# First norm of a two-layer decoder step: all squares on ScalarE behind the token splits, and half of the first key products in other PSUM banks

## The chip, the core and the metric

The kernel runs on one core of a Trainium2 chip. The metric is the device time of one execution in microseconds. Three runs of the kernel before gave 1672.52 us at the median (1671.01 to 1674.88). The engines are TensorE (PE, with its weight loads PEld), VectorE (DVE), ScalarE (ACT), GpSimd (POOL) and SyncE (SP), which here issues nearly all DMAs. Each works through its own instructions strictly in order.

## The reference

One inference step of a trunk of two layers for 512 prompt tokens and 32 sample tokens that share the weights. Only the start matters here:

```python
def rms_norm(x, g):
    y = xf * lax.rsqrt(jnp.mean(xf * xf, axis=-1, keepdims=True) + RMS_EPS)
    return (y * g).astype(x.dtype)

for l in range(DEPTH):
    hp = rms_norm(xp, norm_mix[l]); hs = rms_norm(xs, norm_mix[l])
    if l % 2 == 0:
        z, xbc, dt, q, k, v = even_split(hp @ w_in_even[li])
        ...   # state space branch, sliding-window attention, output projection
    else:
        ...   # forgetting attention
    ...       # cross-attention, SwiGLU
```

Layer 0 is the even one: its norm is the first norm, and the keys `k`, the values `v` (computed together with `dt`) and the queries `q` are its first projections.

## The kernel before

Tokens lie along the free axis: 544 of them (512 and 32), in two chunks of 256 and 288 columns (`CH`), called c0 and c1. The 1024 model features are eight tiles k0 to k7 of 128 partitions; k0 to k3 and k4 to k7 sit in two buffers each ("halves"). All products are done in 32-bit: each operand is split into a high part (a cast to `fp32r`, ACT) and a low part (the rest, DVE), and `acc3` (L187, its matmuls recorded at L138) issues three matmuls for each k: high by high, high by low, low by high. For activations `split` (L248) makes `xh` at L258 and `xl` at L259; for weights `wpiece` (L161) loads a piece of 512 KB into one of two raw buffers, L169 makes the high and L170 the low part. `vpieces` (L174) does the same for the value weights (L182, L183).

The norm's gain is put into the split; the factor 1/rms comes later, at the eviction from PSUM. For it the squares of all eight k are added into `acc`, TensorE sums each over the partitions by matmuls with one column (`rstd`, L290), DVE scales the sum (L302), POOL raises it to the power -0.5 (L303, called the power below), TensorE spreads it over the partitions (the matmuls on `room,col`), and DVE copies that to SBUF (L310). Only then can the key products be evicted (L462).

`first` (L392) is the opening. Its DMAs are tied into one order: x of c0, k0 to k3; key weights 0; x of c0, k4 to k7; key weights 1; x of c1 in two halves; the table of constants `cst`. Each x load is followed by four splits. Then `setup_copies` makes 16-bit copies of the identity and of the mask on DVE (L371, L372), and a loop over c0 and c1 makes the squares: those of c0 by POOL (L429), those of c1 by ACT (L431) through two buffers `sq`, all additions by POOL (L433). `norm_end` stands in `with self.ahead(m0)`, which gives it the priority of the kernel's start.

`even` (L644) goes on: `linear` makes the keys (two weight pieces by two chunks, 24 matmuls each), the value products follow (five blocks of tokens, 24 matmuls with 272 columns each), then the queries. A product takes one PSUM bank; the pool gives four banks to the tag `tr`, three to `sc` (the attention's scores), two to `tp`, one to `pv`. Keys and values all use `tr`.

The program text sets priorities only: `build` opens the context with `schedule_with_timeline_sim=True`, and the scheduler orders each engine's instructions by a timeline of its own. `after` (L451) adds a dependence that holds for this order alone, without a semaphore. So an edit at the start can also reorder instructions far behind it. The stretch concerned here is the end of the state space branch at 330 to 420 us: the prompt's scan (L870 to L903), the sample's state update (L991 loads the state into `hb`, POOL scales it at L1002, DVE adds at L1003, L1004 stores it), and beside it the split of the memory tokens (`mem`, `memh`, `meml`) and their keys.

Of the kernel before, what the change touches and what calls it, by code (L numbers as in the profile page):

```python
# [9 lines left out]
F32 = mybir.dt.float32  # L10
# [4 lines left out]
AF = mybir.ActivationFunctionType  # L15
ALU = mybir.AluOpType
# [3 lines left out]
P = 128  # L20
D = 1024
KD = 8
# [24 lines left out]
C_ID, C_U, C_L, C_ONE, C_SWA, C_MS, C_MN = 0, 128, 256, 384, 512, 768, 896  # L47
C_UB, C_LB, C_S4, C_BLK, C_OH, C_PW, C_END = 1024, 1056, 1088, 1120, 1128, 1144, 1145
# [58 lines left out]
class Net:  # L107
# [79 lines left out]
    def acc3(self, ps, whi, wlo, xhi, xlo, first, last):  # L187
        self.mm(ps, whi, xhi, first, False)
        self.mm(ps, whi, xlo, False, False)
        self.mm(ps, wlo, xhi, False, last)  # L190

    def linear(self, get, ns, KT, xh, xl, evac, tail=0, lead=0, order=(0, 1)):

        for _ in self.linear_steps(get, ns, KT, xh, xl, evac, tail, lead, order):
            pass

    def linear_steps(self, get, ns, KT, xh, xl, evac, tail=0, lead=0, order=(0, 1), tag="tr"):
        def run(n, c, w):
            o, N = CH[c]
            ps = self.psum(tag, [P, 288])  # L200
            for k in range(KT):
                self.acc3(ps[:, 0:N], w[0][:, k], w[1][:, k], xh[k][:, o:o + N], xl[k][:, o:o + N],
                          k == 0, k == KT - 1)
            evac(n, c, ps[:, 0:N])
        ns = list(ns)
        groups = [ns[:lead]] if lead else []
        groups += [[n] for n in ns[lead:len(ns) - tail]]
        groups += [ns[len(ns) - tail:]] if tail else []
        for g in groups:
            ws = [get(n) for n in g]  # L210
            for c in order:
                for n, w in zip(g, ws):
                    run(n, c, w)
                    yield
# [152 lines left out]
    def setup_copies(self):  # L367
        nc, c = self.nc, self.cst
        self.identb = self.keep(64).bitcast(BF16)
        self.maskb = self.keep(128).bitcast(BF16)  # L370
        nc.vector.tensor_copy(self.identb, self.ident)  # L371
        nc.vector.tensor_copy(self.maskb, c[:, C_SWA:C_SWA + 256])  # L372
        self.half = self.keep(60)
        nc.vector.tensor_scalar(self.half, self.par[:, V_CW:V_CW + 60], 0.5, None, ALU.mult)
        self.nsink = self.keep(17)
        nc.vector.tensor_scalar(self.nsink, self.par[:, V_SK:V_SK + 17], -1.0, None, ALU.mult)
# [15 lines left out]
    def first(self):  # L392

        nc, I = self.nc, self.I
        self.x = Big(self, "x")
        st = self.norm_begin(G_MIX)
        m0 = self.mark()
        d = None

        def load(*a):  # L400
            nonlocal d
            e = nc.sync.dma_start(*a)
            d = self.after(e, d) if d is not None else e

        def x_in(c, m):
            o, N = CH[c]
            load(self.x.half(m)[:, :, o:o + N], I["x"][:, 4 * m:4 * m + 4, o:o + N])
            for k in range(4 * m, 4 * m + 4):
                self.last = self.split(st["h"], st["l"], self.x[k][:, o:o + N], k, o, N, self.par[:, G_MIX + k:G_MIX + k + 1])
        x_in(0, 0)  # L410
        self.whold = d
        self.early = self.wpiece(I["we_k"][0], KD, 128)
        d = self.wlast
        x_in(0, 1)
        self.whold = d
        self.early1 = self.wpiece(I["we_k"][1], KD, 128)
        d = self.wlast
        x_in(1, 0)
        x_in(1, 1)
        load(self.cst, I["cst"])  # L420
        self.whold = None
        self.setup_copies()
        for c, (o, N) in enumerate(CH):
            acc = st["acc"][:, o:o + N]
            for k in range(KD):
                x = self.x[k][:, o:o + N]
                sq = acc if k == 0 else self.pers.tile([P, 288], F32, tag="sq", bufs=2, name=self.nm("sq"))[:, 0:N]
                if c == 0:
                    nc.gpsimd.tensor_tensor(sq, x, x, ALU.mult)  # L429
                else:  # L430
                    nc.scalar.activation(sq, x, AF.Square)  # L431
                if k:
                    nc.gpsimd.tensor_tensor(acc, acc, sq, ALU.add)  # L433
            with self.ahead(m0):
                self.norm_end(st, c)
        return st

    def mark(self):
# [205 lines left out]
    def even(self, st, nxt, fill):  # L644
        nc, tc, I, O = self.nc, self.tc, self.I, self.O
        with ExitStack() as es:
            ev = es.enter_context(tc.tile_pool(name="even", bufs=1))
            kT = ev.tile([P, 2, NT], F32, name="kT")
# [3 lines left out]
            dtA = ev.tile([P, 5, 16], F32, name="dtA")  # L652
            craw = ev.tile([P, 12, 27], F32, name="craw")
            xh, xl = st["h"], st["l"]
            self.linear(lambda n: self.early1 if n else self.early, range(2), KD, xh, xl, self.scale_evac(lambda n: kT[:, n], st["b"]))

            wv = self.vpieces(I["we_v"])
            nc.gpsimd.memset(dt, 0.0)
            for i, (o, w) in enumerate(TB):
                ps = self.psum("tr", [P, 288])  # L660
                for k in range(KD):
                    whi, wlo = wv[k // 4][0][:, k % 4], wv[k // 4][1][:, k % 4]
                    a, b = xh[k][:, o:o + w], xl[k][:, o:o + w]
# [19 lines left out]
            with tc.tile_pool(name="swa", bufs=1) as self.sw, tc.tile_pool(name="conv", bufs=1) as cv:  # L683
# [11 lines left out]
                m0 = self.mark()  # L695
# [11 lines left out]
            with tc.tile_pool(name="ssm", bufs=1) as sm:  # L707

                oh, ol = Big(self, "oh", F32R), Big(self, "ol", F32R)
                for c in range(2):  # L710
                    o, N = CH[c]
# [79 lines left out]
    def ssm(self, xs, BC, dt, dtA, sm):  # L791
        nc, I, O = self.nc, self.I, self.O
# [11 lines left out]
        oh = sm.tile([P, 16], F32R, name="ohs")  # L804
        self.zero(cs2.bitcast(F32))
        self.zero(ecs2.bitcast(F32))
        nc.vector.tensor_copy(oh, self.cst[:, C_OH:C_OH + 16])
        self.after(nc.vector.tensor_copy(sel, self.cst[:, C_OH:C_OH + 16].rearrange("p (j r) -> p j r", r=2).unsqueeze(3).to_broadcast([P, 8, 2, 64])), self.last)
        hs_ = sm.tile([P, 2048], F32, name="hst")
        h, csT, ecsT = hs_[:, 0:1024], hs_[0:16, 1024:1536], hs_[0:16, 1536:2048]  # L810
        ps = self.psum("tp", [P, 512])
# [8 lines left out]
        ps = self.psum("tp", [P, 4, 64])  # L820
# [9 lines left out]
        for c in range(4):  # L830
            o = 128 * c
            tok = slice(o, o + 128)
            xx = self.H("xdt")[:, 0:2048].rearrange("p (s h x) -> p s h x", s=2, h=16)
# [3 lines left out]
            ps = self.psum("tp", [P, 4, 128])  # L837
# [6 lines left out]
            for g in range(2):  # L844
                ps = self.psum("tp", [P, 8, 64])
# [6 lines left out]
            for g in range(2):  # L852

                sct = []
                for f in range(2):
# [6 lines left out]
                    for e in range(4):  # L862
                        x = slice(128 * e, 128 * e + 128)
# [13 lines left out]
                for j in range(4):  # L877
                    x = xs[4 * g + j][:, tok]
# [1005 lines left out]
```

## Time and profile before

| | |
|---|---|
| median of three runs | 1672.52 us |
| the profiled execution | 1674.47 us, its span 1672.7 us |
| PE, PEld busy | 1630.3 us (97%), 1522.7 us (91%) |
| DVE, ACT, POOL busy | 1195.0, 795.4, 339.7 us |
| the key products | first matmul at 7.68 us, last begins at 29.02 us |
| the value products and the two sums beside them | 31.02 to 49.34 us |
| first query product | at 49.34 us |

The profile page gives totals by engine, and one digit (tenths of busy time) for each fortieth of the span, here 41.8 us long. The trace answers narrower questions: who waited for whom, the timeline of one engine with the idle time before an instruction in brackets, the chain of waits, and the busy time, granted clock and DMA share of chosen stretches. A PE row's length is modelled and overlaps the next row, so a matmul's cost is read from the distance of the starts.

### The profile page before, as it was taken

How to read it: one execution, taken by the hardware profiler on the slowest of the kernel's cores; microseconds unless marked ns; L12 is line 12 of the kernel's file. 1: busy time of each engine (PE TensorE's matmuls, PEld its weight loads, DVE VectorE, ACT ScalarE, POOL GpSimd, SP SyncE). 2: the span in 40 equal slices, each digit the busy share in tenths (PEclk: the TensorE clock that was granted, in tenths of full speed). 3: DMA queues.
4: the chain of work that ended last, by engine and by line, in shares of the span. 5: the costliest groups of instructions: out<-in, count | busy, mean ns of one | idle time of the engine just before them, and what ended most of it. 6: DMA issues, size and time to landing. Idle time of an engine off the chain costs nothing.

```text
span 1672.7 us, 32467 instructions
## 1 busy us (share of the span) xinstructions
PE 1630.3 (97%) x12720; PEld 1522.7 (91%) x12720; DVE 1195.0 (71%) x2322; ACT 795.4 (48%) x1637; POOL 339.7 (20%) x511
## 2 busy tenths in 40 slices
PE   7999999999999999999999998998999999999998
PEld 6999999877998999999999995655989999999997
DVE  6678889777776876767666577655667886767654
ACT  4367645344545444444445265544545444444434
POOL 6022323675422300000002203111313200000002
PEclk9999999998999999999999999999999999999999
DMA  5121243156433242323224434555451232323222
GB/s 188 56 64 52 83 153 130 39 183 223 160 115 115 64 131 91 101 89 110 80 77 136 133 108 122 161 165 190 139 190 51 94 112 92 104 87 108 76 71 85
DMA packets 71221, 189.27 MB, mean 113 GB/s; under 512 B 7612, under 2 KB 34012, under 8 KB 63452
## 3 DMA queue, kind: packets, MB, share of 16 engines
q1 hardware_dynamic: 69932, 185.43, 33.7%
q8 instruction: 100, 1.64, 0.4%
q10 hardware_dynamic: 1056, 1.24, 0.3%
q0 software_dynamic: 80, 0.52, 0.1%
q14 instruction: 53, 0.43, 0.1%
HBM read 172.22 MB, written 14.95 MB: 112 GB/s over the span
## 4 chain that ended last, share of the span: by engine, by line
PE 90%; DVE 3%; POOL 2%; issue 2%; DMA 1%; ACT 1%; SPq 0%; POOLq 0%; DVEq 0%; ACTq 0%
PE ps L138 65%; PE ps L1594 22%; PE ps L141 3%; POOL room L433 1%; DMA o_s_ssm<-hb 0%; DVE meml L259 0%; DVE xs L910 0%; POOL sq L429 0%; ACT prt L1192 0%; DVE prt L1191 0%; SPq L1268 0%; POOL E L870 0%; DMA room<-wo_d 0%; DMA x<-x 0%; DVE ol L256 0%
## 5 line engine op out<-in xcount | busy, mean ns | idle before, releaser
L138 PE MATMUL ps<-xh,split_t 128*128 128x288 f32 (+1 forms) x2304 | 464.5, 294 | 9.6 <-ACT split_t L169 7.7
L138 PEld LDWEIGHTS ps<-xh,split_t 128*128 128x128 f32 x2304 | 372.4, 191 | 11.9 <-ACT split_t L169 7.7
L1594 PE MATMUL ps<-xf,split_t 128*128 128x272 f32 x2592 | 350.4, 289 | 0.1
L138 PE MATMUL ps<-xl,split_t 128*128 128x256 f32 (+1 forms) x1152 | 339.4, 295 | 1.1 <-DVE xl L259 1.0
L1594 PEld LDWEIGHTS ps<-xf,split_t 128*128 128x128 f32 x2592 | 335.9, 188 | 0.5 <-DVE split_t L1575 0.5
L268 POOL TENSOR_TENSOR room<-room,sq 128x256 f32<-128x256 f32 (+1 forms) x96 | 87.2, 912 | 771.4 <-ACT sq L267 769.8
L138 PEld LDWEIGHTS ps<-xl,split_t 128*128 128x128 f32 x1152 | 219.6, 191 | 3.5 <-DVE xl L259 1.9
L138 PE MATMUL ps<-hh,fs 128*128 128x256 f32 (+1 forms) x1024 | 209.4, 290 | 3.6 <-DVE fs L1640 3.6
L169 ACT CAST split_t<-room 128x1024 fp32r<-128x1024 f32 (+1 forms) x128 | 130.3, 1019 | 154.2 <-PE ps L138 116.9
L170 DVE TENSOR_TENSOR split_t<-room,split_t 128x1024 fp32r<-128x1024 f32 (+1 forms) x128 | 159.1, 1245 | 33.5 <-ACT split_t L169 32.8
L138 PEld LDWEIGHTS ps<-hh,fs 128*128 128x128 f32 x1024 | 166.5, 190 | 4.3 <-DVE fs L1640 4.0
L1574 ACT CAST split_t<-fr 128x1024 fp32r<-128x1024 f32 x108 | 113.5, 1052 | 111.8 <-PE ps L1594 52.6
L1575 DVE TENSOR_TENSOR split_t<-fr,split_t 128x1024 fp32r<-128x1024 f32 x108 | 131.8, 1220 | 37.2 <-ACT split_t L1574 36.9
L138 PE MATMUL ps<-hl,fs 128*128 128x256 f32 (+1 forms) x512 | 147.9, 290 | 0.0
L138 PE MATMUL ps<-oh,split_t 128*128 128x288 f32 (+1 forms) x512 | 105.5, 295 | 1.3 <-ACT oh L253 1.2
L138 PEld LDWEIGHTS ps<-hl,fs 128*128 128x128 f32 x512 | 97.0, 190 | 0.0
L138 PEld LDWEIGHTS ps<-oh,split_t 128*128 128x128 f32 x512 | 82.1, 188 | 6.2 <-ACT oh L253 3.0
L138 PE MATMUL ps<-ol,split_t 128*128 128x288 f32 (+1 forms) x256 | 75.4, 294 | 0.3 <-DVE ol L256 0.2
L259 DVE SCALAR_TENSOR_TENSOR xl<-x,room,xh 128x256 fp32r<-128x256 f32 (+1 forms) x96 | 69.7, 755 | 5.4 <-ACT xh L258 5.4
L138 PE MATMUL ps<-hh,split_t 128*128 128x256 f32 (+1 forms) x384 | 73.5, 289 | 0.0
L1639 ACT CAST fs<-room 128x512 fp32r<-128x512 f32 x64 | 39.6, 619 | 67.1 <-PE ps L138 58.9
L1575 DVE TENSOR_TENSOR fs<-fr,fs 128x512 fp32r<-128x512 f32 x36 | 24.9, 691 | 64.9 <-ACT fs L1574 64.9
(427 smaller groups left out, 3158.2 us busy)
## 6 DMA issues: line engine op xcount, KB each, us to landing
fr<-wfi SPq DMA_DIRECT2D x36, 1024.0 KB
room<-wfo SPq DMA_DIRECT2D x64, 256.0 KB
room<-wo_e SPq DMA_DIRECT2D x16, 512.0 KB
xk<-mem_k SPq DMA_DIRECT2D x8, 1024.0 KB
xv<-mem_v SPq DMA_DIRECT2D x8, 1024.0 KB
room<-wfi SPq DMA_DIRECT2D x16, 512.0 KB
fox_k<-fox_k SPq DMA_DIRECT2D x64, 128.0 KB
fox_v<-fox_v SPq DMA_DIRECT2D x64, 128.0 KB
```

Of the source, the lines that this page charges most:

```text
L138: return self.placed(self.nc.tensor.matmul(out, lhsT, rhs, start=start, stop=stop))
L141: return self.placed(self.nc.tensor.transpose(out, in_, self.ident[0:k, 0:k]))
L169: nc.scalar.copy(hi[:, 0:n], raw[:, 0:n])
L170: nc.vector.tensor_tensor(lo[:, 0:n], raw[:, 0:n], hi[:, 0:n].bitcast(F32), ALU.subtract)
L259: return nc.vector.scalar_tensor_tensor(ll, src, g, hh.bitcast(F32), ALU.mult, ALU.subtract)
L268: nc.gpsimd.tensor_tensor(acc, acc, sq[:, 0:N], ALU.add)
L433: nc.gpsimd.tensor_tensor(acc, acc, sq, ALU.add)
L1574: nc.scalar.copy(hi, t)
L1575: nc.vector.tensor_tensor(lo, t, hi.bitcast(F32), ALU.subtract)
L1594: self.nc.tensor.matmul(ps, w[a][:, k], x[:, b, k], start=start and k == 0 and i == 0, stop=k == 3 and i == 2, skip_group_check=True)
L1639: nc.scalar.copy(hi, raw)
```

## The change

Squares: POOL's multiplications go. All sixteen squares are made by ACT, into `xx`, which has a place for each k, and they are tied behind the last split of the tokens (`self.last` is the last `xl`); the order of the additions on POOL is tied from c0 to c1, and `norm_end` loses its raised priority. The two 16-bit copies and the small copy `ohs`, which belongs to a later stage, are tied behind `self.last` too. Keys: `lead=2` makes `linear` take both weight pieces together, so that the order is c0 of both, then c1 of both, and the first two products take banks with the tag `sc`, the other two `tr`.

```diff
-    def linear(self, get, ns, KT, xh, xl, evac, tail=0, lead=0, order=(0, 1)):
+    def linear(self, *a, **k):
...
-            ps = self.psum(tag, [P, 288])
+            ps = self.psum(tag() if callable(tag) else tag, [P, 288])
...
-        nc.vector.tensor_copy(self.identb, self.ident)
-        nc.vector.tensor_copy(self.maskb, c[:, C_SWA:C_SWA + 256])
+        self.after(nc.vector.tensor_copy(self.identb, self.ident), self.last)
+        self.after(nc.vector.tensor_copy(self.maskb, c[:, C_SWA:C_SWA + 256]), self.last)
...
+        xx = Big(self, "xx")
         for c, (o, N) in enumerate(CH):
             acc = st["acc"][:, o:o + N]
             for k in range(KD):
-                x = self.x[k][:, o:o + N]
-                sq = acc if k == 0 else self.pers.tile([P, 288], F32, tag="sq", bufs=2, name=self.nm("sq"))[:, 0:N]
-                if c == 0:
-                    nc.gpsimd.tensor_tensor(sq, x, x, ALU.mult)
-                else:
-                    nc.scalar.activation(sq, x, AF.Square)
+                sq = xx[k][:, o:o + N] if k else acc
+                self.after(nc.scalar.activation(sq, self.x[k][:, o:o + N], AF.Square), self.last)
                 if k:
-                    nc.gpsimd.tensor_tensor(acc, acc, sq, ALU.add)
-            with self.ahead(m0):
-                self.norm_end(st, c)
+                    i = nc.gpsimd.tensor_tensor(acc, acc, sq, ALU.add)
+                    if c and k == 1:
+                        self.after(i, summed)
+                    summed = i
+            self.norm_end(st, c)
...
-            self.linear(lambda n: self.early1 if n else self.early, range(2), KD, xh, xl, self.scale_evac(lambda n: kT[:, n], st["b"]))
+
+            turn = iter(("sc", "sc", "tr", "tr"))
+            self.linear(lambda n: self.early1 if n else self.early, range(2), KD, xh, xl, self.scale_evac(lambda n: kT[:, n], st["b"]), lead=2,
+                        tag=lambda: next(turn))
...
-        nc.vector.tensor_copy(oh, self.cst[:, C_OH:C_OH + 16])
+        self.after(nc.vector.tensor_copy(oh, self.cst[:, C_OH:C_OH + 16]), self.last)
```

ScalarE in the opening, before. `xh` of 288 columns are the splits of c1, L431 the squares, `vh` the value weights, `split_t` the pieces of key and query weights.

```order
L258 ACTIVATE xh_81<-x_79,room 128x288 x4
L431 ACTIVATE room<-x_79 128x288
L258 ACTIVATE xh_96<-x_94,room 128x288 x4
L431 ACTIVATE sq_164<-x_79 128x288
L431 ACTIVATE sq_167<-x_79 128x288
L182 CAST vh_310<-vr_309 128x1088
L431 ACTIVATE sq_170<-x_79 128x288
```

The same place after the change (lines have moved by a few; L428 are the squares).

```order
L258 ACTIVATE xh_81<-x_79,room 128x288 x4
L258 ACTIVATE xh_96<-x_94,room 128x288 x4
L428 ACTIVATE room<-x_79 128x256
L428 ACTIVATE xx_133<-x_79 128x256 x3
L428 ACTIVATE xx_140<-x_94 128x256 x4
L428 ACTIVATE room<-x_79 128x288
L428 ACTIVATE xx_133<-x_79 128x288 x3
L428 ACTIVATE xx_140<-x_94 128x288 x4
L169 CAST split_t<-room 128x1024
L182 CAST vh_298<-vr_297 128x1088
L169 CAST split_t<-room 128x1024
L182 CAST vh_298<-vr_297 128x1088
```

The sixteen squares stand in one run behind the splits, and the first value weights behind them and behind the first query piece.

TensorE between the last key product and the first value products, before. `ps_283` is the last key product, `room,col_78` spreads the factor of c0, `128x2x128` adds the attention's mask into a bank of scores, `128x1` are the sums of the squares of c1, `ps_319` is the first value block.

```order
L138 MATMUL ps_159<-room,col_78 128x128 x2
L138 MATMUL ps_283<-xh_96,split_t 128x288
L138 LDWEIGHTS room
L138 MATMUL ps_1441<-room 128x2x128
L138 LDWEIGHTS room
L138 MATMUL ps_1468<-room 128x2x128
L138 LDWEIGHTS room
L138 MATMUL ps_1501<-room 128x2x128
L138 MATMUL ps_185<-room 128x1 x3
L138 MATMUL ps_319<-vh_310,xh_81 128x272
L138 MATMUL ps_319<-vh_310,xl_82 128x272
L138 MATMUL ps_319<-vl_311,xh_81 128x272
```

After the change, the same place. `ps_271` is the last key product, `ps_149` the sums of c0, `ps_307` and `ps_334` the first two value blocks.

```order
L138 MATMUL ps_271<-xh_96,split_t 128x288
L138 LDWEIGHTS room
L138 MATMUL ps_1429<-room 128x2x128
L138 MATMUL ps_149<-room 128x1 x2
L138 MATMUL ps_307<-vh_298,xh_81 128x272
L138 MATMUL ps_307<-vh_298,xl_82 128x272
L138 MATMUL ps_334<-vh_298,xh_81 128x272
L138 MATMUL ps_334<-vh_298,xl_82 128x272
L138 MATMUL ps_307<-vl_299,xh_81 128x272
```

The sums of c1 have left this place: they and two of the three masks stand behind the first two value blocks now, and the spread of c0's factor stands inside these, after 28 value matmuls. The first value block has changed places with them and waits for the value weights alone.

SyncE in the state space branch, before. `wxk` are weight pieces for the memory keys, `hb` the sample's state, `o_p_ssm` the store of the prompt's final state, `mem` the memory tokens.

```order
L165 DMA room<-wxk 128x1024 x3
L991 DMA hb_4377<-state 128x1024 x2
L991 DMA hb_4487<-state 128x1024 x2
L903 DMA o_p_ssm<-hst 128x1024
L165 DMA room<-wxk 128x1024
L991 DMA hb_4626<-state 128x1024 x2
L1338 DMA mem_4643<-mem 128x512 x4
```

And after.

```order
L165 DMA room<-wxk 128x1024 x2
L905 DMA o_p_ssm<-hst 128x1024
L165 DMA room<-wxk 128x1024
L993 DMA hb_4365<-state 128x1024 x2
L993 DMA hb_4475<-state 128x1024 x2
L165 DMA room<-wxk 128x1024
L993 DMA hb_4614<-state 128x1024 x2
```

The store and one weight piece have moved ahead of the first four loads of the state; on DVE the addition on which the store waits has moved ahead of the products `sxdt` (L949) too.

## Rows read from the trace of the kernel before

**Rows 1.** The page: busy time by engine, and TensorE's granted clock in forty slices (9 is 0.9 or more).

```profile
PE 1630.3 (97%) x12720; PEld 1522.7 (91%) x12720; DVE 1195.0 (71%) x2322; ACT 795.4 (48%) x1637; POOL 339.7 (20%) x511
PEclk9999999998999999999999999999999999999999
```

**Rows 2.** The chain of waits, cut off at 60 us: start, length, what.

```profile
28.43 0.79 POOL room L433
...
31.02 29.09 PE ps L138 x217
```

**Rows 3.** Stretches of the opening: length, then busy time (and instructions) of PE, PEld, DVE, ACT and POOL, granted clock, DMA share, GB/s.

```profile
10.40:15.85 5.45, 5.42 (x25) 5.43 (x26) 5.45 (x6) 3.85 (x9) 5.29 (x7) 1.00 1.04 420
15.85:22.70 6.85, 5.77 (x41) 5.04 (x40) 6.85 (x11) 4.55 (x8) 6.09 (x7) 1.00 0.34 115
22.70:26.10 3.40, 3.34 (x14) 3.34 (x15) 3.40 (x6) 2.12 (x4) 1.61 (x1) 0.50 0.02 5
29.50:32.90 3.40, 2.11 (x18) 1.88 (x16) 1.99 (x5) 1.04 (x1) 2.16 (x3) 1.00 0.43 154
32.90:36.30 3.40, 3.40 (x18) 3.40 (x17) 0.29 (x1) 0.00 (x0) 1.01 (x1) 0.51 0.50 154
```

**Rows 4.** TensorE's timeline: start, length, instruction, in brackets the idle time before it and what ended it.

```profile
7.68 0.58 PE L138 MATMUL ps<-xh,split_t 128*128 128x256 f32 x1 [7.68 <-ACT split_t L169]
10.43 0.80 PE L138 MATMUL ps<-xh,split_t 128*128 128x256 f32 x2 [1.95 <-DVE split_t L170]
12.94 0.41 PE L138 MATMUL ps<-xl,split_t 128*128 128x256 f32 x1
13.58 0.41 PE L138 MATMUL ps<-xl,split_t 128*128 128x256 f32 x1
16.29 0.28 PE L138 MATMUL ps<-xl,split_t 128*128 128x256 f32 x1
16.64 0.27 PE L138 MATMUL ps<-xl,split_t 128*128 128x256 f32 x1
22.76 0.61 PE L138 MATMUL ps<-xl,split_t 128*128 128x288 f32 x1 [0.81 <-DVE xl L259]
27.72 0.29 PE L138 MATMUL ps<-xl,split_t 128*128 128x288 f32 x1
28.12 0.29 PE L138 MATMUL ps<-xl,split_t 128*128 128x288 f32 x1
29.02 0.38 PE L138 MATMUL ps<-xh,split_t 128*128 128x288 f32 x1
29.23 0.50 PE L138 MATMUL ps<-room 128*128 128x256 bf16 x3
31.02 0.83 PE L138 MATMUL ps<-room 128*128 128x1 f32 x6 [1.29 <-POOL room L433]
49.34 0.28 PE L138 MATMUL ps<-xh,split_t 128*128 128x256 f32 x1
```

**Rows 5.** DVE's timeline in the opening, same columns.

```profile
8.74 1.63 DVE L170 TENSOR_TENSOR split_t<-room,split_t 128x1024 fp32r<-128x1024 f32 x1
10.29 3.33 DVE L259 SCALAR_TENSOR_TENSOR xl<-x,room,xh 128x256 fp32r<-128x256 f32 x4
22.20 0.94 DVE L259 SCALAR_TENSOR_TENSOR xl<-x,room,xh 128x288 fp32r<-128x288 f32 x2
24.33 1.27 DVE L183 TENSOR_TENSOR vl<-vr,vh 128x1088 fp32r<-128x1088 f32 x1
25.53 2.35 DVE L170 TENSOR_TENSOR split_t<-room,split_t 128x1024 fp32r<-128x1024 f32 x2
```

**Rows 6.** ACT's timeline: the first weight splits, the last split of the tokens, the value weights, and two runs of squares from later stages (256 and 288 columns).

```profile
9.36 1.03 ACT L169 CAST split_t<-room 128x1024 fp32r<-128x1024 f32 x1
12.61 1.80 ACT L258 ACTIVATE xh<-x,room 128x288 fp32r<-128x288 f32 x4
18.76 1.09 ACT L182 CAST vh<-vr 128x1088 fp32r<-128x1088 f32 x1
377.94 1.62 ACT L267 ACTIVATE sq<-mem 128x256 f32<-128x256 f32 x5
422.75 1.43 ACT L267 ACTIVATE sq<-xs 128x288 f32<-128x288 f32 x4
```

**Rows 7.** POOL's timeline: the power of c0, an addition run, the power of c1, and a power with DVE idle.

```profile
24.49 3.97 POOL L303 TENSOR_TENSOR col<-col,room 128x2 f32<-128x2 f32 x1 [2.24 <-DVE col L302]
28.43 2.54 POOL L433 TENSOR_TENSOR room<-room,sq 128x288 f32<-128x288 f32 x3
389.20 0.71 POOL L303 TENSOR_TENSOR room<-room 128x2 f32<-128x2 f32 x1
```

**Rows 8.** The state space branch: SP's issues, POOL's run over the state, and TensorE's wait for the memory tokens.

```profile
321.18 24.56 SPq L165 DMA_DIRECT2D room<-wxk  x3
356.80 3.19 SPq L991 DMA_DIRECT2D hb<-state  x4
362.43 0.33 SPq L165 DMA_DIRECT2D room<-wxk  x1
364.97 13.79 POOL L1002 TENSOR_TENSOR hb<-hb,CmYi 128x512 f32<-128x512 f32 x12 [1.37 <-PE ps L138]
379.78 0.58 PE L138 MATMUL ps<-meml,split_t 128*128 128x256 f32 x1 [4.75 <-DVE meml L259]
```

More of the change, by code (lines that the diff above doesn't have):

```diff
@@ L190, in acc3 @@
         self.mm(ps, wlo, xhi, False, last)
-    def linear(self, get, ns, KT, xh, xl, evac, tail=0, lead=0, order=(0, 1)):
-        for _ in self.linear_steps(get, ns, KT, xh, xl, evac, tail, lead, order):
+    def linear(self, *a, **k):
+        for _ in self.linear_steps(*a, **k):
             pass
@@ L396, in first @@
         st = self.norm_begin(G_MIX)
-        m0 = self.mark()
         d = None
```

## The prediction

> **What bounds the kernel now.** I read the page first: TensorE is busy 97% of the span at a granted clock of 0.9 or more in every slice [rows 1]. So a microsecond counts if TensorE idles in it or runs at its lower level, and the only place that this change touches on purpose is the opening, before the first query product at 49.34 [rows 4]. Second, the chain of waits: until 31.02 it runs over POOL's additions of squares, from there over TensorE [rows 2]. Third, the stretches, and fourth the timelines of the engines, which show four losses.
>
> - TensorE begins at 7.68, and after three matmuls waits 1.95 us for the low part of the first key weights. It runs on from 10.43 [rows 4]. Till about 15.8 three matmuls of 256 columns take 0.64 us (12.94 to 13.58), later 0.35 (16.29 to 16.64): 0.213 and 0.117 each, the levels of 1.2 and 2.4 GHz. The stretch view prints 1.00 there [rows 3]; the distances decide.
> - Between 15.85 and 22.70 TensorE is busy 5.77 of 6.85 us [rows 3]: it waits for low parts `xl`, the longest time 0.81 us before 22.76 [rows 4], because DVE has copies ahead of the last two.
> - The granted clock is 0.50 from 22.70 to 26.10 and 0.51 from 32.90 to 36.30, each time behind a stretch with idle time [rows 3]. Each costs half of 3.4, 1.7 us.
> - Before 31.02 TensorE stands 1.29 us for the last sum of c1 [rows 4], which POOL ends late: the power of c0 took 3.97 us against 0.71 where DVE was idle, since DVE was at work until 27.88, and three additions (2.54) come behind it [rows 5, 7].
>
> **The change part by part.**
>
> DVE. The four `xl` of c0 took 3.33 us beside POOL's multiplications and additions, 0.83 each; the two at 22.20, with POOL idle, 0.94, so 0.47. A low part of weights took 1.63 beside POOL, and 2.35 for two without it, 1.2 each [rows 5]. POOL now has nothing until the first squares come, at about 14.9. High weights 0 are ready just before 7.68, as today [rows 4]; low weights 0 then at 8.9 instead of 10.37, low weights 1 (high part 10.39 [rows 6]) at 10.7 + 1.2 = 11.9 instead of about 15.2 (the `xl` run ends at 13.62, and 1.63 follow), and the eight `xl` of c1, at 0.47 or at the pace of ACT, at about 15.6 instead of 23.14. The `xl` waits go, since TensorE needs these later than that in the new order.
>
> Keys. 94 of the 96 matmuls follow from 8.9. Where the clock rises I can't know: today it rose 5.4 us after the matmuls became continuous [rows 3, 4]. I take 12.4 as the early end (slow for 3.4 us, as in both later stretches [rows 3]) and 15.8, where it rose today, as the late one. Early: 16 matmuls at 0.213 to 12.4, the other 30 of 256 columns at 0.117 (3.5 us), 48 of 288 columns at 0.133 (27.72 to 28.12 for three [rows 4]) 6.4: 22.3. Late: 32 till 15.8, then 1.6 and 6.4: 23.8. Today the last begins at 29.02 and ends its 0.21 later [rows 4]. So the keys end 5.4 to 6.9 us earlier.
>
> ACT. The splits of c1 end at 14.1 (today 14.41, with one square of 0.3 to 0.4 between [rows 6]). Then sixteen squares: a run of 256 columns costs 1.62 for five, 0.32, a run of 288 columns 1.43 for four, 0.36 [rows 6]; 8 x 0.32 + 8 x 0.36 = 5.4, to 19.5. What queues behind them is the first query piece (1.03) and the value weights (1.09 [rows 6]): high parts at about 21.6 (today 19.85) and 23.5, low parts on DVE at 23.4 to 23.8 and 26.6 to 27.0 (with 1.63 beside the additions, 1.27 without). The squares therefore cost nothing while the keys end at 22.3 or later; without that cover each square would cost its 0.3.
>
> POOL. Seven additions for c0 at 0.85 (2.54 for three [rows 7]) from 14.9: done at 20.8, before the keys end. Four for c1 stand before the power of c0: 24.3. DVE's scaling of the sum must wait for TensorE's sums behind the keys, 23 to 24.5; behind it DVE runs a query piece and the second value weights, 2.5 us. The wait this adds stands at the spread of c0, on TensorE, with 20 matmuls of the same two value blocks and all later ones queued behind it. Bounds: nothing, if the power slips in at once (0.71); 2 us, if it has to wait for DVE's run, as it did at 24.49, and DVE goes on with the third query piece. TensorE gets to the spread at 26.4 to 28, and by the first run DVE is through at about 27, so I take 0.3.
>
> Values. Today the sums of c1 and all values take 31.02 to 49.34, 18.3 us with one slow stretch; 16.6 at the full clock. After: they start with the low value weights at 23.5 to 24.3, and the spread of c0 and a mask or two come on top, 0.6 by the 0.50 of three masks [rows 4]. They end at 40.7 to 41.5, with 0.3 for the spread 41 to 41.8. Two of the three banks of scores are now held by keys; the masks that need them stand 6 us behind, past the eviction, at no cost. Against 49.34 that is 7.5 to 8.3. A slow stretch may follow if TensorE idles long enough around 23.5 or at the spread: 0 to 1.7; I take 0.8. Gain at the first query: about 7 us. On the bad side, with 2.0 at the spread (1.7 more than taken) and one whole slow stretch, 7.5 - 1.7 - 1.7 = 4.1; with two, 2.4.
>
> A DVE instruction of the opening lost about 0.4 us beside POOL: 0.83 against 0.47, 1.63 against 1.2 [rows 5]. The Trainium skill, "SBUF — State Buffer", section "Who interferes with whom", says that a DVE instruction with two inputs in SBUF and a GpSimd instruction that reads SBUF shut each other out for a whole instruction. Taken to its end, each of DVE's two splits between 20.5 and 24 would lose a whole addition, 0.85 and not 0.4, and the values would start 0.9 us later: 1666.4 by the rule, 1665.5 by the rows.
>
> The rest. Behind the opening TensorE is the bound and nothing is tied to the clock on the wall, so the gain moves on. The scheduler also reordered 330 to 420 us, where TensorE waits 4.75 us for the memory tokens [rows 8]. That wait may vanish (-4.75), or grow by 2 to 3 us; today POOL's run over the state, twelve times 1.15, ends at 378.76 and then the wait ends [rows 8]. This run's inputs move little in either direction, so I take 0, and 2 us on both sides for the range.
>
> Sum: -7.0. The profiled execution took 1674.47 (span 1672.7), 1.95 above the median; taken off both, 1667.5 for such an execution, and 1672.5 - 7.0 = 1665.5 for the median.
>
> **Rivals.**
>
> A. The power of c0 becomes the bound. For it: 3.97 us at 24.49 in the very place that DVE is busy again. Against it: TensorE comes to the spread 3.5 us after the first values, not at once. Price: late keys, the 2.0 at the spread, two slow stretches, and 0.9 for splits beside more of POOL's additions: 2.4 - 0.9 = 1.5, so 1671.0, no change that can be told.
>
> B. Slower: SyncE. The first load of the state is issued at 356.80; now a store and a weight load stand ahead of it. If that weight load gets its raw buffer only when today's load at 362.43 gets one [rows 8], the state comes 6 us late, and 1.3 to 2.5 more for the up to 1 MB ahead of it at 420 GB/s [rows 3], and POOL's run and the wait for the memory tokens move with it: 7.3 to 8.5, say 8.1, and two slow stretches more, 3.4. -7.0 + 8.1 + 3.4 = +4.5: 1677.0. Slower by over 0.2% needs a state that is 7 us late. Against it: the load at 362.43 is the next piece; the moved one was issued by 345.74 today [rows 8], so its buffer is free by then, and the addition on which the store waits has moved up too.
>
> C. The change does what it says, and the time is lost again: at the memory tokens TensorE arrives 7 us earlier and waits longer for data that comes when it came. 1672.5. Against it: the state's loads are released by TensorE's own transposes and move with it.
>
> **How the numbers follow.** Two medians of this kernel can be told apart from about 0.2%, 3.3 us: 1669.2 to 1675.8 counts as the same. The forecast has 0.75 and is faster throughout, A has 0.12 and C 0.05, both within 0.2%, together 0.17, and B 0.08. The forecast's own range is 1662 to 1669 (8.3 and 2 for the late stage on one side; 4.1 less some of those 2 on the other). The range asked for takes in A, to 1671.5, and starts at 1661 for a late wait that shrinks further. That leaves out B, C and a part of A, with the far ends some 0.2.
>
> **What would show it.** Right: low weights 0 end near 8.9, the eight `xl` near 15.6; TensorE without a wait for `xl`; last key near 22 to 24; first low value weights near 23.5; no wait of more than 0.5 us at the spread; first query at 41 to 43; granted clock 1.00 from the keys on. Wrong: `vh` later than the keys' end by over a microsecond (squares dearer than 0.36), a power of 3 us or more with TensorE behind it, a stretch at 0.50 behind 24, a first query after 45, or a wait for `meml` above 6 us.

## The result and the profile after

The changed kernel takes 1676.64 us (median of 22 runs) against 1671.99 for the kernel before (22 runs): ratio 1.0024, 95% interval 1.0014 to 1.0034, so about 4 us slower, where 1665.5 was forecast. The profiled execution took 1675.93, span 1674.2 (before 1674.47 and 1672.7). The page looks as before [rows 1]: the loss lies in two places that only the closer views show. The two profiled executions differ by 1.46 us, less than the medians (4.65), so these traces hold only a part of it.

**The opening.** TensorE's timeline of the changed kernel answers to [rows 4]:

```profile
9.04 0.80 PE L138 MATMUL ps<-xh,split_t 128*128 128x256 f32 x2 [0.46 <-DVE split_t L170]
...
22.46 0.29 PE L138 MATMUL ps<-xh,split_t 128*128 128x288 f32 x1
22.60 0.62 PE L138 MATMUL ps<-room 128*128 128x256 bf16 x5
23.08 0.37 PE L138 MATMUL ps<-vh,xh 128*128 128x272 f32 x1
...
29.94 1.22 PE L138 MATMUL ps<-room,col 128*128 128x128 f32 x4 [3.08 <-POOL col L303]
...
45.28 0.28 PE L138 MATMUL ps<-xh,split_t 128*128 128x256 f32 x1
```

The last key stands at 22.46 instead of 29.02 and the first value at 23.08 instead of 31.71, with no wait between. Then TensorE stands 3.08 us at the spread of c0, for the power. The stretches behind it, as in [rows 3], show the clock:

```profile
26.10:29.50 3.40, 0.77 (x7) 0.55 (x5) 2.47 (x2) 0.00 (x0) 3.32 (x3) 1.00 0.38 145
29.50:32.90 3.40, 2.96 (x13) 2.96 (x14) 1.18 (x3) 0.00 (x0) 2.74 (x4) 0.54 0.52 154
```

The granted clock is 0.54 for the 3.4 us behind the wait, half speed. The first query product comes at 45.28, 4.06 us ahead of before. Why the power was late stands in POOL's and DVE's timelines (the second fence shows pairs of additions out of that run of eleven; compare [rows 5, 7]):

```profile
14.88 14.34 POOL L430 TENSOR_TENSOR room<-room,xx 128x256 f32<-128x256 f32 x11 [11.53 <-ACT xx L428]
29.18 0.71 POOL L303 TENSOR_TENSOR col<-col,room 128x2 f32<-128x2 f32 x1
```

```profile
17.07 1.55 POOL L430 TENSOR_TENSOR room<-room,xx 128x256 f32<-128x256 f32 x2
...
22.09 3.60 POOL L430 TENSOR_TENSOR room<-room,xx 128x288 f32<-128x288 f32 x2
```

```profile
15.29 0.28 DVE L372 CAST room<-room 128x256 bf16<-128x256 f32 x1
20.29 1.23 DVE L170 TENSOR_TENSOR split_t<-room,split_t 128x1024 fp32r<-128x1024 f32 x1 [4.72 <-ACT split_t L169]
21.44 1.83 DVE L183 TENSOR_TENSOR vl<-vr,vh 128x1088 fp32r<-128x1088 f32 x1
23.26 0.16 DVE L302 TENSOR_SCALAR col<-ps 128x2 f32<-128x2 f32 x1
23.34 1.68 DVE L170 TENSOR_TENSOR split_t<-room,split_t 128x1024 fp32r<-128x1024 f32 x1
24.94 1.90 DVE L183 TENSOR_TENSOR vl<-vr,vh 128x1088 fp32r<-128x1088 f32 x1
26.76 1.81 DVE L170 TENSOR_TENSOR split_t<-room,split_t 128x1024 fp32r<-128x1024 f32 x1
```

While DVE stands idle, to 20.29, an addition takes 0.78 us; beside DVE's splits it takes 1.7 to 1.9, and all splits but the first take 1.7 to 1.9 instead of 1.2. The eleven additions took 14.34 us, 1.30 each. DVE had the power's input ready at 23.42, but three more additions of c1 stood ahead in POOL's queue, and it ran at 29.18.

**The late stage.** TensorE's waits between 160 and 440 us, first before, then after (what it waited for, us in total, times, longest):

```profile
PE ps L138 <- DVE meml L259: 4.8, 1, 4.8
PE ps L138 <- DVE eb L890: 0.6, 1, 0.6
```

```profile
PE ps L138 <- DVE meml L259: 3.7, 1, 3.7
PE ps L138 <- DVE eb L892: 2.2, 1, 2.2
PE ps L138 <- POOL room L303: 1.1, 1, 1.1
PE ps L138 <- DVE sR L978: 0.3, 1, 0.3
PE ps L138 <- DMA hb<-state: 0.2, 1, 0.2
PE ps L138 <- DVE hb L1005: 0.2, 1, 0.2
```

The wait for the memory tokens shrank, but `eb` of the state space branch is waited for 2.2 us, and there is a new wait for a power, that of the memory tokens' norm. To see where time went, take one weight split on ScalarE that stands at the same place in every order, and ask how far ahead of the kernel before it starts. The last column of the table, ratio and interval, is the timing; the others come from single traces, which later also differ by slow stretches that fall differently in each execution.

| lead over before, us | first query (49.34) | split at 183.30 | split at 432.74 | split at 572.78 | median, ratio [interval] |
|---|---|---|---|---|---|
| changed kernel | 4.06 | 4.03 | -0.56 | -0.70 | 1676.64, 1.0024 [1.0014, 1.0034] |
| 1 no tie on ohs | 6.13 | 6.10 | -1.12 | -1.15 | 1675.57, 1.0017 [1.0003, 1.0031] |
| 2 only the tie | -0.46 | -0.49 | -7.81 | -7.93 | 1679.53, 1.0032 [1.0015, 1.0049] |
| 3 power first | 8.61 | 8.58 | 3.44 | 3.28 | 1672.76, 0.9998 [0.9984, 1.0012] |
| 4 power first, no tie | 8.69 | 8.66 | 6.80 | 6.76 | 1670.67, 0.9989 [0.9975, 1.0003] |
| 5 both powers first, no tie | 9.34 | 9.32 | 5.02 | 4.98 | 1666.28, 0.9954 [0.9934, 0.9973] |
| 6 memory's power first, no tie | 4.26 | 4.23 | 0.57 | 0.53 | 1671.90, 0.9989 [0.9975, 1.0003] |
| 7 squares alone | -2.00 | -2.00 | -3.89 | -3.92 | 1679.63, 1.0040 [1.0027, 1.0053] |
| 8 keys alone | 4.54 | 4.52 | 5.32 | 5.30 | 1671.80, 0.9991 [0.9978, 1.0004] |
| 9 both powers first, with tie | 8.22 | 8.19 | 4.89 | 4.72 | 1670.65, 0.9981 [0.9967, 0.9996] |

The changed kernel holds its 4 us to 183 us and loses 4.6 by 433. (The before-runs beside the experiments had medians of 1672.89 to 1673.68; compare ratios.)

### The profile page after: what moved, and what is told of

Read it like the earlier page. It is cut to its first block, busy times and chain, and to the rows that moved or that the text cites. A ratio compares the mean times of both kernels' runs of the same rounds, so it can differ in the third digit from the quotient of the medians.

```text
span 1674.2 us, 32476 instructions
## 1 busy us (share of the span) xinstructions
PE 1630.7 (97%) x12720; PEld 1522.7 (91%) x12720; DVE 1189.9 (71%) x2322; ACT 798.0 (48%) x1645; POOL 332.5 (20%) x503
## 3 DMA queue, kind: packets, MB, share of 16 engines
q8 instruction: 100, 1.64, 0.4%
## 4 chain that ended last, share of the span: by engine, by line
PE 90%; DVE 3%; ACT 2%; issue 2%; DMA 1%; SPq 1%; POOL 1%; DVEq 0%; POOLq 0%; ACTq 0%
PE ps L138 65%; PE ps L1596 22%; PE ps L141 3%; SPq L1270 1%; DMA x<-x 0%; POOL room L430 0%; SPq L1266 0%; DVE meml L259 0%; DVE xs L912 0%; ACT xh L258 0%; DMA mem<-mem 0%; DMA room<-wo_d 0%; ACT xx L428 0%; DVE sR L978 0%; DVE prt L1193 0%
## 5 line engine op out<-in xcount | busy, mean ns | idle before, releaser
L258 ACT ACTIVATE xh<-x,room 128x256 fp32r<-128x256 f32 (+1 forms) x96 | 48.2, 517 | 47.5 <-DVE x L323 28.0
```

The source lines that it names most:

```text
L258: nc.scalar.activation(hh, src, AF.Copy, scale=g)
```

## The experiments

**1 and 2: the tie on `ohs`.** One line of the change lets a constant, `ohs`, be made only behind the last split. Built without it, the changed kernel has the order of before from 190 to 430 us except for small pieces; the kernel before with that line alone has the changed kernel's. Experiment 1 is the changed kernel with

```diff
-        self.after(nc.vector.tensor_copy(oh, self.cst[:, C_OH:C_OH + 16]), self.last)
+        nc.vector.tensor_copy(oh, self.cst[:, C_OH:C_OH + 16])
```

> The changed kernel without one tie: the copy that makes the constant ohs may stand anywhere again. The opening is the changed kernel's, instruction for instruction, and between 190 and 430 us the order is that of the kernel before but for a few transposes. Theory 1 (the gain of the opening, 4.1 us at the first query, is given back by the new order between 190 and 430 us, which this tie brings about): about 1668, ratio 0.9975 against before; the first query at 45.3 as in the changed kernel, and at 440 us still 3 to 4 us ahead of before. Theory 2 (the late order is neutral; the opening itself leads to more time later, through the clock or through transfers that come too late for it): 1676 to 1677, ratio 1.002 to 1.003, like the changed kernel.

Measured 1.0017, near what theory 2 says. But the trace shows the gain of the opening kept to the split at 366.05 in before (6.19 ahead) and lost between there and 433, in the memory tokens' norm. TensorE and POOL there, then the granted clock, and last POOL at this place in the kernel before:

```profile
387.50 1.22 PE L138 MATMUL ps<-room 128*128 128x128 f32 x4 [3.24 <-POOL room L303]
```

```profile
378.48 0.91 POOL L268 TENSOR_TENSOR room<-room,sq 128x256 f32<-128x256 f32 x1
381.52 4.27 POOL L268 TENSOR_TENSOR room<-room,sq 128x256 f32<-128x256 f32 x4 [2.14 <-ACT sq L267]
385.75 1.69 POOL L303 TENSOR_TENSOR room<-room 128x2 f32<-128x2 f32 x1
```

```profile
385.00:390.00 5.00, 2.50 (x10) 2.41 (x11) 3.04 (x5) 0.20 (x1) 3.87 (x4) 0.62 0.63 175
390.00:395.00 5.00, 5.00 (x24) 3.11 (x24) 2.24 (x4) 1.46 (x2) 1.05 (x1) 0.70 0.32 88
```

```profile
384.63 0.91 POOL L268 TENSOR_TENSOR room<-room,sq 128x256 f32<-128x256 f32 x1
387.68 1.55 POOL L268 TENSOR_TENSOR room<-room,sq 128x256 f32<-128x256 f32 x2 [2.14 <-ACT sq L267]
```

It is the opening's picture again: DVE had the power's input ready at 380.64, but five additions of the gated norm stand ahead of it, four of them still to run; in the order of before there are three, and the power at 389.20 was in time [rows 7]. So neither theory was complete. (Single openings scatter: this one waited 1.88 us at the spread and led by 6.1 at the first query, that of experiment 6, the same instructions in the same order, 2.46 and 4.3.)

Experiment 2 is the kernel before with the same line the other way round.

> The kernel before with that one tie on ohs and nothing else. The opening is that of before, the order from 190 to 430 us that of the changed kernel. Theory 1: slower than before by what the changed kernel loses there, 4.6 us in the profiles and up to 8 by the medians: 1677 to 1680, ratio 1.003 to 1.005. Theory 2: as before, 1672, ratio 1.000.

Measured 1.0032, 5.4 us. The opening is that of before and 7.3 us are lost between 183 and 433. `eb` is waited for 2.2 us, a power 2.2. Theory 1 holds for this half, though these two waits are not the whole 7.3.

**3 and 4: the power of c0 first.** The changed kernel with

```diff
-        e = nc.gpsimd.tensor_tensor(cc, cc, self.cst[:, C_PW:C_PW + 1].to_broadcast([P, n]), ALU.pow)
+        e = self.power = nc.gpsimd.tensor_tensor(cc, cc, self.cst[:, C_PW:C_PW + 1].to_broadcast([P, n]), ALU.pow)
...
-                        self.after(i, summed)
+                        self.after(i, self.power)
```

> The changed kernel with the first addition of c1 tied behind the power of c0, so that POOL has no addition of c1 between the last one of c0 and this power; the late order stays that of the changed kernel. If the wait of 3.08 us at the spread and the slow stretch behind it come from the four additions that stand ahead of the power: no wait at the spread, first query 3 to 4.5 us earlier than the changed kernel (41 to 42), time 1672 to 1673.5, ratio 1.000 to 1.001 if theory 1 holds. Rival: the seven additions of c1, each 1.7 us beside DVE, now end later than TensorE wants their sums, and the wait only moves to the sums of c1: first query at 44 to 45, 1676.

Measured 0.9998, 4 us better than the changed kernel. The first query stands at 40.73 and TensorE does not wait at the spread:

```profile
14.75 7.23 POOL L430 TENSOR_TENSOR room<-room,xx 128x256 f32<-128x256 f32 x7 [11.41 <-ACT xx L428]
23.73 1.64 POOL L303 TENSOR_TENSOR col<-col,room 128x2 f32<-128x2 f32 x1 [1.75 <-DVE col L302]
```

The seven additions take 7.23, and the power follows its input at once. Experiment 4 adds the edit of experiment 1.

> Both edits together: the power of c0 ahead of the additions of c1, and no tie on ohs (late order of before). Theory 1 with the power as the opening's loss: 1664 to 1665, ratio 0.9955, about what I had forecast for the change. Theory 1 with the wait only moved to the sums of c1: 1668. Theory 2: 1672 or more.

Measured 0.9989, with an interval that takes in 1: 2 us by the ratio, 3 by the medians, and not the 7.5 expected. Again a wait of 2.77 us for the memory tokens' power: 8.76 ahead at 366, 6.80 at 433.

**5 and 6: the same at the second place.** The memory's power is kept, and the gated norm's second addition tied behind it:

```diff
-            self.rstd(acc, self.mcol, self.mb, [(0, 0, 128), (1, 128, 128)])
+            self.mpow = self.rstd(acc, self.mcol, self.mb, [(0, 0, 128), (1, 128, 128)])[2]
...
-            nc.gpsimd.tensor_tensor(acc, acc, sq[:, 0:N], ALU.add)
+            self.added = nc.gpsimd.tensor_tensor(acc, acc, sq[:, 0:N], ALU.add)
...
             self.norm_tile(yn, y, j, c)
+            if c == 0 and j == 2:
+                self.after(self.added, self.mpow)
```

Experiment 5 has this, the power of c0 first and no tie; experiment 6 this and no tie.

> The kernel with the power of c0 first and no tie on ohs, and the same edit at the second place: the memory tokens' power, behind which TensorE stood 2.8 us at 380.8, comes ahead of all but one of the additions of the gated norm on POOL. Theory 3 (a power that POOL's queue holds back behind additions of another block costs its wait on TensorE, at both places): no wait for the power there, 1667 to 1668, ratio 0.997. Rival (the memory tokens set the pace there, and the wait only moves to the next thing, or the clock takes it): 1670 to 1671, ratio 0.999.

> The changed kernel without the tie on ohs, and with the memory tokens' power ahead of all but one of the gated norm's additions; the opening stays the changed kernel's with its late power of c0. Theory 3: the 3.24 us at the memory tokens' spread and the slow stretch behind it (granted 0.62 and 0.70 for 10 us) go: 1669.5 to 1672.5, ratio 0.998 to 0.999. Rival as for the kernel with both powers first: stays at 1675 to 1676, ratio 1.0015.

Measured 0.9954 and 0.9989: 1666.28 (seven runs) is the fastest version, faster than both kernels, and 6 gained 3.7 us on 1 by the medians. POOL in experiment 5:

```profile
375.23 0.91 POOL L268 TENSOR_TENSOR room<-room,sq 128x256 f32<-128x256 f32 x1
376.56 0.71 POOL L303 TENSOR_TENSOR room<-room 128x2 f32<-128x2 f32 x1 [0.43 <-DVE room L302]
378.27 1.55 POOL L268 TENSOR_TENSOR room<-room,sq 128x256 f32<-128x256 f32 x2 [0.99 <-ACT sq L267]
```

Neither trace has a wait for this power any more, and by the times theory 3 holds at both places. But the traces also show what the rival says, a wait that moves on: in both, TensorE now stands for a third power, that of the gated norm, for which 1 and 4 do not wait. POOL, DVE and TensorE of experiment 5 there, then TensorE of 6:

```profile
410.63 3.43 POOL L303 TENSOR_TENSOR col<-col,room 128x2 f32<-128x2 f32 x1 [14.37 <-DVE col L302]
```

```profile
410.48 3.03 DVE L912 SCALAR_TENSOR_TENSOR xs<-zs,xs 128x288 f32<-128x288 f32 x8
```

```profile
414.12 1.04 PE L138 MATMUL ps<-room,col 128*128 128x128 f32 x4 [2.26 <-POOL col L303]
```

```profile
418.58 0.71 PE L138 MATMUL ps<-room,col 128*128 128x128 f32 x4 [3.14 <-POOL col L303]
```

No addition stands ahead of this power: it lasts as long as DVE's eight instructions run without a gap. Taking that away was not tried. So between 183 and 433 the lead lost shrinks from 7.2 us in experiment 1 to 3.7 in 6, but grows from 1.9 in 4 to 4.3 in 5. The profiled execution of 5, 1670.44 us, is the slowest of its seven; where the faster ones gain their time, and so how much of the gain is the memory tokens' power, no trace shows.

**7 and 8: the parts alone.** The kernel before with the diff's part on the squares, and with its part on the keys:

```diff
+        xx = Big(self, "xx")
...
+                self.after(nc.scalar.activation(sq, self.x[k][:, o:o + N], AF.Square), self.last)
```

> The kernel before with only the part on the squares: all sixteen on ScalarE behind the last split of the tokens, the additions on POOL behind them. Three additions of c1 stand ahead of the power of c0. Reading by the opening: DVE runs without POOL beside it till 15 us, low weights 0 near 9, the eight xl of c1 near 15 to 16, so the whole gain of the opening comes from here; first query at 44 to 46, a wait of 1 to 3 us at the spread; time 1668 to 1672 if the late order, which is nearly that of before, takes nothing away, and 1673 to 1676 if the memory tokens' power is late again.

```diff
+            turn = iter(("sc", "sc", "tr", "tr"))
...
+                        tag=lambda: next(turn))
```

> The kernel before with only the part on the keys: both key pieces of c0 first, then c1, half of them in banks of the attention. The squares stay on POOL and DVE beside it, so the low parts come as late as before: first query at 49 to 50. Theory 3: the time is that of before, 1672 to 1674, if the memory tokens' power is ready, 2 to 3 us more if it is late (the order there changes in 60 places on TensorE). Rival (the keys' order carries the gain of the opening): first query at 45, 1668.

Both expectations of the opening fell. Squares alone are slower than before, 1.0040, and the first query comes at 51.34; keys alone give 4.54 us there. TensorE in experiment 7, then in 8:

```profile
22.76 0.29 PE L138 MATMUL ps<-xh,split_t 128*128 128x288 f32 x1
22.89 0.84 PE L138 MATMUL ps<-room 128*128 128x256 bf16 x7
27.81 1.23 PE L138 MATMUL ps<-room,col 128*128 128x128 f32 x4 [4.08 <-POOL col L303]
32.20 1.44 PE L138 MATMUL ps<-room 128*128 128x1 f32 x6 [3.17 <-POOL room L430]
```

```profile
26.56 0.61 PE L138 MATMUL ps<-room,col 128*128 128x128 f32 x4
26.92 0.38 PE L138 MATMUL ps<-xh,split_t 128*128 128x288 f32 x1
27.14 0.28 PE L138 MATMUL ps<-vh,xh 128*128 128x272 f32 x1
```

With the squares alone the keys end 6.3 us earlier, and then no value product follows: by the program's tags four key results hold the four `tr` banks until the spread lets them go, and TensorE stands 4.08 and 3.17 us for POOL's chain. With half of the keys in `sc` banks, value products follow the keys directly. So the part on the keys is what the opening's gain cannot do without; the early end of the keys is worth something only with that cover and with a power in time (8.6 in experiment 3). The order and the banks were not built apart; the keys end as early in 7, in the old order, which speaks for the banks. The time of 8 alone, 0.9991, is no difference that can be told: its trace keeps the lead to 572.78 (5.30), but its span, 1671.7 us, is only 1.0 shorter than before, and where the rest went was not followed.

**9: the late order by itself.** Experiment 5 with the tie put back (the line of experiment 1 left as the change has it).

> The whole change, its tie on ohs put back, with both powers ahead of the additions: the same as the kernel with both powers first but for the late order, which the tie decides. Theory 1, as it now stands (the late order costs by itself, with a wait of 2.2 us for eb and some more between 190 and 440 us, whatever the opening and the powers do): 4 to 6.5 us slower than the kernel with both powers first, 1670.5 to 1673, ratio 0.999 to 1.000; eb waited for 2.2 us and no wait for a power at the memory tokens. Rival (the 4.6 us that the changed kernel lost late were the late powers, and the late order is neutral once they are first): 1666 to 1667, ratio 0.9955.

Measured 0.9981, 4.4 us slower than experiment 5 by the medians. No power is waited for at the memory tokens, `eb` 2.2 us:

```profile
320.26 0.33 PE L138 MATMUL ps<-cs,ohs 128*128 128x128 f32 x1 [2.22 <-DVE eb L892]
```

Theory 1 holds here too, at the lower edge of the time that it expected (the ratio is below its 0.999), and the rival's 0.9955 lies outside the interval. In the single traces the two kernels stand only 0.1 us apart at 433 (4.89 and 5.02), since 5 has the third power's wait there and 9 has not; so the price of the late order rests on the medians of 9 against 5 and of 2 against before, and only 1.7 us of it (2.22 less 0.56) is pinned to a wait.

## Why the prediction was wrong

- *DVE, keys and ACT: right.* Low weights 0 ended at 8.98 (8.9 forecast), the last `xl` at 15.24 (15.6), the keys at 22.75 (22.3 to 23.8), the squares at 19.32 (19.5); the first low value part was used at 23.67 (23.5 to 24.3).
- *POOL, the term of the spread: wrong size, 3.08 for 0.3, beyond my upper bound of 2.* The step that failed is "seven additions for c0 at 0.85 ... four for c1 ...: 24.3". I took 0.85 from three additions that ran when DVE had ended its splits at 27.88, and charged the collision to DVE's splits alone. POOL's additions more than doubled (0.78 to about 1.8), and the power stood in their queue, not merely behind a DVE run. The Trainium skill, "SBUF — State Buffer", section "Who interferes with whom", calls the port that DVE and GpSimd share an exclusive lock, on which one side blocks outright for a whole instruction of the other. Taken in turn, an addition of 0.78 and a split of 1.22 would take 2.0 each; the trace has 1.7 to 1.9 for both, so it nearly agrees, and for both engines, where I had applied it to one. With 1.6 us for the slow stretch (3.4 us at 0.54) against the 0.8 taken, the gain at the first query was 4.06 for 7. Experiments 3 and 5, with the power in time, have 8.6 and 9.3: the rest of that sum, 7.5 to 8.3, was not too large. (A slip of reading beside it: before its wait of 1.95 us TensorE had issued two matmuls, as the "94 of the 96" has it, not three.)
- *Rival A: what happened in the opening*, with 3.08 for its 2.0; the 4.1 that I had as the forecast's bad side matches the 4.06 measured in part by luck, for the wait was a microsecond longer than in that sum and the rest of the gain about as much larger. Two signs of being wrong came: the stretch at 0.54, and a first query after 45. I gave the rival 0.12 because TensorE would come to the spread 3.5 us after the first values; it came 3.8 us after them, and the power 3 us later still.
- *The rest, "I take 0": the larger error.* I saw the reorder from 330 to 420 us, looked at its memory tokens and its state loads, and left out its other waits, and I did not ask which line of the diff brought it about. It is a tie on a constant that does no work in the opening. By the timings it costs 4.4 (9 against 5, whose intervals overlap a little) to 5.4 us (2 against before). In the two other pairs, the changed kernel against 1 and 3 against 4, the ratios give it only 1.2 and 1.5 us, within the noise: without the tie the memory tokens' power comes late there (3.24 and 2.77 us). So the changed kernel loses the time late with the tie or without it, by two different causes, and what the order costs beyond the wait for `eb` stays open.
- *Rivals B and C: no.* The wait for `meml` fell from 4.75 to 3.66, TensorE waits 0.2 us for the state. The slower time has another mechanism than B, whose 1677.0 is near the 1676.64 measured by chance.
- *What earns the gain.* I gave it to the relief of DVE and gave the keys' banks no part in it. Experiments 7 and 8 correct this: squares alone cost 0.4%, and the part on the keys makes the gain possible (4.54 us at the first query by itself); the part on the squares, with the relief of DVE, adds about 4 us to that only where the power is in time (8.6 in experiment 3).

## What to carry to other kernels

Where a short instruction that TensorE waits for shares a queue with a long run of others, order it ahead explicitly, and read its time from rows in which the neighbouring engine does what it will do in the new kernel. When a scheduler orders the program, price every reordered stretch by its own waits, and find by building single lines which one causes it: a tie on a constant that the opening does not use reordered the whole stage from 190 to 430 us here. An early end of one stage is a gain only if the next has a bank and an input to start with.

## What was not expected of the hardware

A two-column power on POOL, 0.71 us with DVE idle, took 3.43 us in all eleven traces where eight DVE instructions ran without a gap beside it (3.03 us), as if it were let in only behind the last. It is not always so: in experiment 3 the power of c0 took 1.64 us, from 23.73 on, and ended 0.58 us behind the first of two splits that follow each other on DVE:

```profile
23.57 1.22 DVE L170 TENSOR_TENSOR split_t<-room,split_t 128x1024 fp32r<-128x1024 f32 x1
24.71 1.28 DVE L183 TENSOR_TENSOR vl<-vr,vh 128x1088 fp32r<-128x1088 f32 x1
```

What tells the two cases apart is not shown. In long additions and splits the two engines slowed each other about equally.
